# Down projection of a gated hybrid block: 25 instead of 22 groups by seven products, activation forms made after the convolution and read back from HBM, some weight sums added in place

## Chip, cores and metric

One core of one Trainium2 chip. The metric is device microseconds for one launch of the whole block; lower is better. The profile is one execution of the kernel on the chip. Engines are called as in it: PE (matmul), PEld (its weight load), DVE (vector), ACT (scalar), POOL (GpSimd), SP (which issues most transfers).

## The reference

One block with sequence 256, model width 2048 and feed-forward width 5632, all in 32-bit floats. Attention in three branches and a gate come first; the change lies in the last third:

```python
h2 = rms_norm(x, g_ffn[l])
u = causal_depthwise_conv(h2 @ w_up[l], conv_w[l], conv_b[l])   # w_up 2048 x 11264, 3 taps
u_gate, u_val = jnp.split(u, 2, axis=-1)
x = x + (jax.nn.silu(u_gate) * u_val) @ w_down[l]               # w_down 5632 x 2048
```

## The kernel before

Every 32-bit operand is split into a high and a low part that the PE reads at full rate: `hi = cast(raw)` on ACT, `lo = raw - hi` on DVE. A product of two split operands takes three matmuls (high by high, low by high, high by low; `three`, lines 1309 to 1311).

*Up projection* (lines 1219 and 1221). 176 pieces of w_up, 512 KB each, are loaded by SP (`piece`, line 172), cast (L175), subtracted (L176) and multiplied with the hidden state `hT`. After each block of rows the convolution runs on ACT and DVE (`conv`); its end is `a = silu(gate) * value`, split into `aT` (44 blocks of 128 rows; the low half at [S:]). `tick` moves such side work on by a step after each piece.

*Weight sums.* During the up projection `weight_sums` also loads w_down for the pairs that will be multiplied "by seven": four loads of 256 KB on SP's queue, three or four DVE additions (L1181), one or two stores of 512 KB to HBM on POOL's queue (L1191, L1193). A new pair starts every 7 pieces. Pairs in `ALL_FOUR` get all four sums T1 to T4 stored (two tiles), the others only T4 and T2.

*Down projection.* The output is made in two halves of 1024 columns (`nb` 0 and 1). The 44 row blocks are taken in 22 pairs per half. A pair is a 2 x 2 block product (two sequence halves t, two row blocks k, two column halves n). Done straight it has 8 products ("e", `eight`): two steps of 12 matmuls. Done by seven ("s", `seven`, Strassen's scheme in Winograd's form) it has 7 products, 21 matmuls, in four steps u0 to u3 of 3, 6, 6 and 6, and it needs

- four *forms* of the activation, sums of its blocks: `forms(p)` (five DVE operations on `aT`, L1273 to L1277, then two casts L1281, L1282 and two subtractions L1284, L1285). It runs as side work during the eights. They are kept in `sf`, in unused places of `aT`, and FS4 in the place of the block that seven products don't need;
- four *sums* of the weight: from HBM (`raw_t<-T`, `t<-T`), or for the pairs outside `ALL_FOUR` two of them added on DVE in step p2 (L1371, L1372).

The plan strings say the order, and with it the order on all queues: loads, casts, subtractions and additions are all held in program order on their engine (`keep`). `AHEAD = 2`: when step i is multiplied, the load and the split of step i+2 are emitted. The buffers are rings, and an entry is written again when its last reader is done:

- `hi` and `lo`: four entries each (`SBUFS`), so the cast of a step can start when the PE has done with the step four before it;
- `raw`: four entries of 512 KB; from the tenth load on each third load goes to `more`, two entries;
- `t13`, two entries, one for each group by seven: T1 and T3 next to each other. T4 and T2 come through `raw` or `more`.

At the end of each half `gather` and `results` add the products to the residual on DVE and store them.

Of the kernel before, what the change touches and what calls it, by code (L numbers as in the profile page):

```python
# [9 lines left out]
F32 = mybir.dt.float32  # L10
# [27 lines left out]
PLANS = ("eeeee" + "se" * 5 + "sse" + "s" + "eee", "e" + "sse" * 4 + "ssse" + "sssee")  # L38
ALL_FOUR = {(0, 6), (0, 7)} | {(1, p) for p in range(14) if p not in (4, 6, 8, 11)}
# [10 lines left out]
NSEVEN = tuple(plan.count("s") for plan in PLANS)  # L50
# [3 lines left out]
def hybrid_block(  # L54
# [1075 lines left out]
    def conv(ps, f, s):  # L1130
# [23 lines left out]
        else:  # L1154
# [9 lines left out]
            ended.append(f)  # L1164

    ended = []
    made = {}
    asked = [(0, p) for p in range(NSEVEN[0])] + [(1, p) for p in range(NSEVEN[1])]

    def weight_sums(nb, p):  # L1170
# [11 lines left out]
        four = (nb, p) in ALL_FOUR  # L1182
        add(r[0][:, 0], r[0][:, 1])
        if four:
            add(r[0][:, 1], r[1][:, 1])
# [3 lines left out]
        made[nb, p] = [dram.tile([P, PIECE], F32, name=f"T{j}_{nb}_{p}") for j in range(1 + four)]  # L1189
        if four:  # L1190
            nc.gpsimd.dma_start(made[nb, p][1], r[0].rearrange("p b n -> p (b n)"))  # L1191
# [15 lines left out]
    for f0 in range(0, FT, 4):  # L1207
        for s in range(2):
            pairs = [two_banks(f"u{f0 + i}_{s}") for i in (0, 2)]
            c0 = s * D_FF + f0 * P  # L1210
            for k in range(0, KT, 2):
# [11 lines left out]
                if asked and n_ticks[0] > 8 and n_ticks[0] % 7 == 2:  # L1223
                    adding.append([weight_sums(*asked.pop(0)), 0])
# [22 lines left out]
    FS3, FS1, FS2, FS4 = range(4)  # L1247
# [8 lines left out]
    def form_of(p, f):  # L1256
        if f == FS4:
            return pieces_of(p)[:, 0, :, 1]
        if p < 10:
            return sf[:, p, f]  # L1260
        return pieces_at(31 - p).rearrange("p k (f l q) -> p (k f) l q", f=2, l=2)[:, f]

    def forms(p):

        flat = aT[:, 2 * p : 2 * p + 3].rearrange("p k s -> p (k s)").bitcast(F32)
        v = flat[:, :1024].rearrange("p (k l t q) -> p k l t q", k=2, l=2, t=NT)
        d = sm.tile([P, 512], F32, tag="junk", bufs=2, name=f"fd_{p}").rearrange("p (f l q) -> p f l q", f=2, l=2)
        r = down_pool().tile([P, 512], F32, tag="fr", bufs=1, name=f"fr_{p}").rearrange("p (f q) -> p f q", f=4)
        g = rbc.rearrange("p (k q) -> p k q", k=2)
        two = flat[:, : 2 * 640].rearrange("p (a b) -> p a b", b=640)[:, :, :512]  # L1270
        two = two.rearrange("p a (l t q) -> p a l t q", l=2, t=NT)[:, :, :, 0]
        tt = nc.vector.tensor_tensor
        keep(tt(d, two, v[:, 0, :, 1].unsqueeze(1).to_broadcast([P, 2, 2, P]), ALU.subtract))  # L1273
# [251 lines left out]
```

## Time and profile before

| | |
|---|---|
| time of three runs | 1473.98, 1471.38, 1471.35 us; median 1471.38 |
| span of the profiled execution (first to last instruction) | 1469.9 us |
| PE busy in the span | 1462.8 us |
| granted TensorE clock, mean | 0.999 |
| up projection, about 755 to 1241 us: PE, DVE, ACT busy | 485.32, 389.15, 337.51 us |
| down projection, about 1241 to 1466 us: matmuls | 990 |

The page names no time for the profiled execution beside its span; the span is 1.5 us below the median of the runs, so what lies around it is about that. A busy PE in the profile means only that matmuls overlap; whether it runs without a gap is read from the distance between the starts of matmuls and from the list of waits.

### The profile page before, as it was taken

Reading aid. Unit: us, or ns where it says so; the run is one execution under the profiler, and the core shown is the slowest. Engines: PE = TensorE matmul, PEld = TensorE weight load, DVE = VectorE, ACT = ScalarE, POOL = GpSimd, SP = SyncE. Lnnn points to the kernel's source line nnn. Section 1 sums busy time; section 2 is a strip of 40 time slices with the busy share of each in tenths; the row PEclk is TensorE's granted clock in tenths of the full one; section 3 lists DMA queues with packets and bytes.
Section 4 is the critical chain, followed back from the end, with each engine's and each line's share of the span. In section 5 each row is a group of like instructions: output and inputs, shape, how many; then the busy total and the mean of one; then the engine's idle time right before and its main releaser. Section 6 shows DMA issues by size and latency. Waiting matters only on the chain.

```text
span 1469.9 us, 20741 instructions
## 1 busy us (share of the span) xinstructions
PE 1462.8 (100%) x7327; PEld 1233.4 (84%) x7327; DVE 1205.1 (82%) x1617; ACT 895.3 (61%) x1287; POOL 68.8 (5%) x139
## 2 busy tenths in 40 slices
PE   9999999999999999999999999999999999999998
PEld 7888888888878888888888888888888888888887
DVE  5798767766997799888877888788887886998998
ACT  6755454454664466545657667567676777665774
POOL 1000001021000000000000000000000010000000
PEclk9999999999999999999999999999999999999999
DMA  8697898787766576866776888889888895778995
GB/s 295 202 341 260 265 313 270 226 294 267 256 221 204 204 271 247 287 222 237 273 239 218 302 272 276 294 277 310 295 265 273 280 305 190 249 256 286 334 315 191
DMA packets 163463, 388.81 MB, mean 265 GB/s; under 512 B 14016, under 2 KB 22512, under 8 KB 163360
## 3 DMA queue, kind: packets, MB, share of 16 engines
q1 hardware_dynamic: 150960, 345.34, 70.6%
q0 software_dynamic: 11648, 41.10, 7.3%
q8 instruction: 57, 0.93, 0.3%
q10 hardware_dynamic: 752, 1.06, 0.2%
q14 instruction: 46, 0.38, 0.1%
HBM read 349.70 MB, written 37.75 MB: 264 GB/s over the span
## 4 chain that ended last, share of the span: by engine, by line
PE 94%; DVE 3%; DMA 2%; issue 1%; ACT 0%; SPq 0%; DVEq 0%; ACTq 0%
PE u L1219 21%; PE u L1221 10%; PE d L1310 5%; PE d L1309 5%; PE d L1311 5%; PE g_x L769 4%; PE g_x L770 4%; PE g_x L771 4%; PE s L186 2%; PE s L188 2%; PE f L187 2%; PE f L188 2%; PE f L186 2%; PE s L187 2%; PE b L186 2%; PE b L188 2%
## 5 line engine op out<-in xcount | busy, mean ns | idle before, releaser
L1219 PE MATMUL u<-hT,hi_u 128*128 128x512 f32 x1408 | 442.6, 396 | 0.0
L1221 PEld LDWEIGHTS u<-hT,lo_u 128*128 128x128 f32 x1408 | 264.4, 188 | 63.5 <-DVE lo_u L176 1.1
L1221 PE MATMUL u<-hT,lo_u 128*128 128x256 f32 x1408 | 277.0, 278 | 0.7 <-DVE lo_u L176 0.7
L176 DVE TENSOR_TENSOR lo_u<-raw_u,hi_u 128x1024 fp32r<-128x1024 f32 x176 | 213.2, 1220 | 59.8 <-ACT hi_u L175 59.0
L175 ACT CAST hi_u<-raw_u 128x1024 fp32r<-128x1024 f32 x176 | 183.0, 1049 | 107.0 <-PE u L1219 54.6
L1219 PEld LDWEIGHTS u<-hT,hi_u 128*128 128x128 f32 x1408 | 214.5, 189 | 0.1
L764 ACT CAST hi_g<-raw_g 128x1024 fp32r<-128x1024 f32 (+1 forms) x96 | 91.1, 964 | 53.5 <-PE g_x L770 33.4
L765 DVE TENSOR_TENSOR lo_g<-raw_g,hi_g 128x1024 fp32r<-128x1024 f32 (+1 forms) x96 | 105.0, 1116 | 20.9 <-ACT hi_g L764 20.8
L769 PE MATMUL g_x<-hi_g,xT 128*128 128x512 f32 x251 | 98.8, 394 | 0.0
L770 PE MATMUL g_x<-hi_g,xT 128*128 128x512 f32 x251 | 97.7, 389 | 0.0
L771 PE MATMUL g_x<-lo_g,xT 128*128 128x512 f32 x251 | 96.3, 390 | 0.0
L1148 DVE TENSOR_TENSOR y<-y,z 128x512 f32<-128x512 f32 x88 | 60.7, 691 | 24.4 <-ACT z L1147 20.5
L1147 ACT ACTIVATE z<-u,taps 128x256 f32<-128x256 f32 x176 | 74.7, 496 | 0.0
L1309 PE MATMUL d<-hi_d,aT 128*128 128x512 f32 x176 | 68.5, 389 | 0.0
L1310 PE MATMUL d<-hi_d,aT 128*128 128x512 f32 x176 | 68.5, 389 | 0.0
L1311 PE MATMUL d<-lo_d,aT 128*128 128x512 f32 x176 | 68.1, 389 | 0.0
L175 ACT CAST hi_f<-raw_f 128x1024 fp32r<-128x1024 f32 (+1 forms) x40 | 38.6, 968 | 46.6 <-PE f L187 41.9
L186 PE MATMUL s<-hi_s,xT 128*128 128x512 f32 (+1 forms) x160 | 61.9, 387 | 0.0
L175 ACT CAST hi_b<-raw_b 128x1024 fp32r<-128x1024 f32 x32 | 33.6, 1052 | 45.2 <-PE b L187 23.5
L175 ACT CAST hi_s<-raw_s 128x1024 fp32r<-128x1024 f32 (+1 forms) x40 | 38.3, 959 | 36.8 <-PE s L187 29.3
L186 PE MATMUL f<-hi_f,xT 128*128 128x512 f32 (+1 forms) x160 | 60.4, 377 | 0.0
L188 PE MATMUL s<-lo_s,xT 128*128 128x512 f32 (+1 forms) x160 | 59.1, 369 | 0.0
(498 smaller groups left out, 3265.0 us busy)
## 6 DMA issues: line engine op xcount, KB each, us to landing
raw_u<-in_w_up_dram SPq DMA_DIRECT2D x176, 512.0 KB, 5.4
raw_g<-in_w_in_dram SPq DMA_DIRECT2D x86, 512.0 KB, 5.4
T<-r POOLq DMA_DIRECT2D x64, 512.0 KB, 6.1
r<-in_w_down_dram SPq DMA_DIRECT2D x88, 256.0 KB, 5.2
raw_d<-in_w_down_dram SPq DMA_DIRECT2D x44, 512.0 KB, 5.4
raw_f<-in_w_in_dram SPq DMA_DIRECT2D x32, 512.0 KB, 5.5
raw_s<-in_w_in_dram SPq DMA_DIRECT2D x32, 512.0 KB, 5.4
raw_s<-in_w_down_dram SPq DMA_DIRECT2D x32, 512.0 KB, 5.3
```

What stands on the lines that cost most here:

```text
L175: pin(nc.scalar.copy(hi[:, :m], raw[:, :m]))
L176: pin(nc.vector.tensor_tensor(lo[:, :m], raw[:, :m], hi[:, :m].bitcast(F32), ALU.subtract))
L186: nc.tensor.matmul(o, lhsT=xh, rhs=wh, start=first, stop=False)
L188: nc.tensor.matmul(o, lhsT=xh, rhs=wl, start=False, stop=last)
L769: nc.tensor.matmul(o, lhsT=a[0], rhs=w[0], start=first, stop=False)
L770: nc.tensor.matmul(o, lhsT=a[1], rhs=w[0], start=False, stop=False)
L771: nc.tensor.matmul(o, lhsT=a[0], rhs=w[1], start=False, stop=last)
L1219: nc.tensor.matmul(ps, lhsT=hi[:, j, c], rhs=hT[:, k + j, :], start=first, stop=False)
L1221: nc.tensor.matmul(ps[:, :S], lhsT=lo[:, j, c], rhs=hT[:, k + j, :S], start=False, stop=last)
L1309: nc.tensor.matmul(o, lhsT=ah, rhs=w[0], start=first, stop=False)
L1310: nc.tensor.matmul(o, lhsT=al, rhs=w[0], start=False, stop=False)
L1311: nc.tensor.matmul(o, lhsT=ah, rhs=w[1], start=False, stop=last)
```

## The change

- 25 pairs are done by seven instead of 22: 10 in the first half, 15 in the second. Letters of the plans: `e` by eight; `f` by seven with both sum tiles read from HBM; `o` by seven with its own sums, added on DVE.
- *Forms.* The five operations on `aT` during the down projection go. After the convolution has made a pair of row blocks, `unsplit_forms` makes the four forms in three DVE operations (over 256, 128 and 128 columns) from the unsplit activation, for the first 15 pairs, and POOL's queue stores them to HBM (256 KB a pair). In the down projection they come back two pairs at a time, 512 KB through the `raw` ring, and are cast and subtracted two pairs at a time: five times in the first half, three times in the second.
- *Weight sums* during the up projection only for the 15 `f` pairs, a new pair every 9 pieces, always with four additions and both stores.
- *`o` pairs.* Their two blocks of w_down are loaded 4 steps (`LEAD`) before their step p0, into a ring `own` of two entries. Four additions make T1 to T4 from them, in program order ahead of p0's split, or one step earlier when an eight stands before the pair.
- *Buffers.* `more` and `t13` go. Both sum tiles of every pair by seven, loaded or added, lie in a new ring `sum` of two entries. `raw` keeps four entries.
- Steps p2 and p3 (with u2 and u3) change places: T1 and T3 first, then T4 and T2.

The core of the diff:

```diff
-PLANS = ("eeeee" + "se" * 5 + "sse" + "s" + "eee", "e" + "sse" * 4 + "ssse" + "sssee")
+PLANS = ("eeeee" + "fofe" + "ofe" * 3 + "o" + "eee", "e" + "offe" * 4 + "off" + "ee")
+LEAD = 4
...
             nc.vector.tensor_tensor(a[:, :, S:], g, a[:, :, :S].bitcast(F32), ALU.subtract)
             ended.append(f)
+            if f // 2 < NFORM:
+                yield 1
+                unsplit_forms(f // 2, g, y)
...
+    def unsplit_forms(p, g, y):
+        v = g.rearrange("p k (t q) -> p (k t) q", t=NT)
+        r = y.rearrange("p k (t q) -> p (k t) q", t=NT)
+        tt = nc.vector.tensor_tensor
+        tt(r[:, :2], v[:, 0:4:3], v[:, 1:2].to_broadcast([P, 2, P]), ALU.subtract)
+        nc.vector.scalar_tensor_tensor(r[:, FS2], r[:, FS1], -1.0, v[:, 0], ALU.mult, ALU.subtract)
+        tt(r[:, FS4], r[:, FS2], v[:, 2], ALU.add)
+        if p % 2 == 0:
+            rforms[p // 2] = dram.tile([P, 2, 512], F32, name=f"rform{p}")
+        nc.gpsimd.dma_start(rforms[p // 2][:, p % 2], y.rearrange("p k s -> p (k s)"))
...
-                if asked and n_ticks[0] > 8 and n_ticks[0] % 7 == 2:
+                if asked and n_ticks[0] > 8 and n_ticks[0] % 9 == 2:
...
-    def buffer(name):
-        turn[0] += 1
-        if turn[0] > 10 and turn[0] % 3 == 0:
-            return down_pool().tile([P, PIECE], F32, tag="more", bufs=2, name=name)
-        return wp.tile([P, PIECE], F32, tag="raw", name=name)
+    def buffer(name, kind):
+        if kind == "raw":
+            return wp.tile([P, PIECE], F32, tag="raw", name=name)
+        return down_pool().tile([P, PIECE], F32, tag=kind, bufs=2, name=name)
...
+    def forms(i):
+        p = 2 * i
+        n = min(2, NFORM - p)
+        raw = load(rforms[i][:, :n].rearrange("p a n -> p (a n)"), f"fr_{i}")
...
+        yield 2
+        keep(nc.scalar.copy(to[:, :, :, 0], r[:, :, :3]))
+        keep(nc.scalar.copy(last[:, :, 0], r[:, :, FS4]))
+        yield
+        keep(nc.vector.tensor_tensor(to[:, :, :, 1], r[:, :, :3], to[:, :, :, 0].bitcast(F32), ALU.subtract))
+        keep(nc.vector.tensor_tensor(last[:, :, 1], r[:, :, FS4], last[:, :, 0].bitcast(F32), ALU.subtract))
...
+    def seven(p, n0, X, Y, first, last, early):
+        own = KINDS[n0 // PIECE][p] == "o"
+        def fetch():
+            for j, k in enumerate((k0, k1)):
+                raw[j] = load(dv[:, k, n0 : n0 + PIECE], f"s{n0}_{k}", "own")
+        def sums():
+            for j in (2, 3):
+                raw[j] = buffer(f"t{j}_{name}", "sum")
+            add = lambda o, a, b: keep(nc.vector.tensor_tensor(o, a, b, ALU.add))
+            add(raw[2][:, :512], raw[0][:, :512], raw[0][:, 512:])
+            add(raw[2][:, 512:], raw[0][:, 512:], raw[1][:, 512:])
+            add(raw[3][:, 512:], raw[1][:, 512:], raw[2][:, :512])
+            add(raw[3][:, :512], raw[1][:, :512], raw[3][:, 512:])
+        if own:
+            before.setdefault(len(steps) - LEAD, []).append(fetch)
+            before.setdefault(len(steps) - early, []).append(sums)
...
         def p2():
-            raw[2] = load(made[n0 // PIECE, p][0], f"t{name}")
-            raw[3] = down_pool().tile([P, PIECE], F32, tag="t13", bufs=2, name=f"t13_{name}")
...
-            w["T4"], w["T2"] = parts(raw[2], f"t42_{name}")
+            if not own:
+                raw[2] = load(made[n0 // PIECE, p][1], f"t13_{name}", "sum")
+                raw[3] = load(made[n0 // PIECE, p][0], f"t42_{name}", "sum")
+            w["T1"], w["T3"] = parts(raw[2], f"t13_{name}")
 
         def p3():
-            w["T1"], w["T3"] = parts(raw[3], f"t13_{name}")
+            w["T4"], w["T2"] = parts(raw[3], f"t42_{name}")
...
+                seven(s, n0, X, Y, s == 0, s == ns - 1, int(plan[i - 1] == "e"))
+                if nb and s % 2 and s // 2 + 5 < (NFORM + 1) // 2:
+                    at(len(steps), lambda i=s // 2 + 5: later(forms(i)))
```

More of the change, by code (lines that the diff above doesn't have):

```diff
@@ L49 @@
 OUT_SEVENS = 3
-NSEVEN = tuple(plan.count("s") for plan in PLANS)
+KINDS = tuple(plan.replace("e", "") for plan in PLANS)
+NSEVEN = tuple(len(kinds) for kinds in KINDS)
+NFORM = max(NSEVEN)
 @with_exitstack
@@ L1188, in weight_sums @@
         add(r[1][:, 0], r[1][:, 1])
[L1189 to L1191 removed]
+        made[nb, p] = [dram.tile([P, PIECE], F32, name=f"T{j}_{nb}_{p}") for j in range(2)]
+        nc.gpsimd.dma_start(made[nb, p][1], r[0].rearrange("p b n -> p (b n)"))
         yield 1
@@ L1297, in load @@
+    def load(src, name, kind="raw"):
+        raw = buffer(f"raw_{name}", kind)
         keep(nc.sync.dma_start(raw[:, : src.shape[1]], src))
         return raw
+    def forms(i):
+        p = 2 * i
+        n = min(2, NFORM - p)
+        raw = load(rforms[i][:, :n].rearrange("p a n -> p (a n)"), f"fr_{i}")
+        r = raw.rearrange("p (a f q) -> p a f q", a=2, f=4)[:, :n]
+        to = sf[:, p % 10 : p % 10 + n]
+        last = aT[:, 2 * p : 2 * (p + n)].rearrange("p (a k) (l t q) -> p a k l t q", k=2, l=2, t=NT)[:, :, 0, :, 1]
+        yield 2
[4 more added lines that the diff above has]
+        keep(nc.vector.tensor_tensor(last[:, :, 1], r[:, :, FS4], last[:, :, 0].bitcast(F32), ALU.subtract))
+        issued.update((f"forms{p}", f"forms{p + 1}"))
@@ L1319, in f_of @@
         return to[:, 0], to[:, 1]
-    steps = []
+    steps, before = [], {}
     def eight(p, n0, X, first, last):
@@ L1348, in eight @@
         steps.append((make(k1), close if last else use(k1)))
-    def seven(p, n0, X, Y, first, last):
+    def seven(p, n0, X, Y, first, last, early):
         k0, k1 = 2 * p, 2 * p + 1
@@ L1381, in u1 @@
         def u1():
+            assert f"forms{p}" in issued
             three(X()[0][0], *a_of(k1, 0), w["10"])
@@ L1460, in hybrid_block @@
             at(-1, lambda: start(0))
+            for i in range(5):
+                at((0, 3, 6, 13, 23)[i], lambda i=i: later(forms(i)))
         for i, c in enumerate(plan):
-            if c == "s":
-                seven(s, n0, X, Y, s == 0, s == ns - 1)
+            if c != "e":
+                seven(s, n0, X, Y, s == 0, s == ns - 1, int(plan[i - 1] == "e"))
+                if nb and s % 2 and s // 2 + 5 < (NFORM + 1) // 2:
+                    at(len(steps), lambda i=s // 2 + 5: later(forms(i)))
                 s += 1
@@ L1471, in hybrid_block @@
                     at(len(steps) - 1, lambda nb=nb: residual(nb))
-                if formed < ns and n_done >= 4 - 3 * nb:
-                    at(len(steps) - 2, lambda p=formed: later(forms(p)))
-                    formed += 1
-        assert s == ns and not straight and formed >= ns
+        assert s == ns and not straight
         at(len(steps) - 1, finish)
@@ L1482, in hybrid_block, with prepare @@
         f()
-    for prep, _ in steps[:AHEAD]:
-        prep()
+    def prepare(j):
+        for f in before.pop(j, []):
+            f()
+        steps[j][0]()
+    for j in range(AHEAD):
+        prepare(j)
     for i, (_, use) in enumerate(steps):
         if i + AHEAD < len(steps):
-            steps[i + AHEAD][0]()
+            prepare(i + AHEAD)
         use()
```

61 lines of the change are left out of this document (13 added, 48 removed).

## The prediction

> **What bounds the kernel now.** I read the page first, then the PE's own waits, then the stages, then single instructions of the down projection.
>
> ```profile
> span 1469.9 us, 20741 instructions
> PE 1462.8 (100%) x7327; PEld 1233.4 (84%) x7327; DVE 1205.1 (82%) x1617; ACT 895.3 (61%) x1287; POOL 68.8 (5%) x139
> ```
>
> The list of waits, for the PE alone, and the one matmul of the up projection that waited:
>
> ```profile
> PE u L1221 <- DVE lo_u L176: 0.7, 1, 0.7
> ...
> 987.82 0.50 PE L1221 MATMUL u<-hT,lo_u 128*128 128x256 f32 x2 [0.68 <-DVE lo_u L176]
> ```
>
> The two halves of the down projection as windows (PE, PEld, DVE, ACT, POOL busy, then clock, DMA share, GB/s), and its matmuls: the count, the first start and the last start.
>
> ```profile
> 755.00:1241.00 486.00, 485.32 (x2788) 423.16 (x2787) 389.15 (x473) 337.51 (x523) 20.28 (x38) 1.00 0.83 275
> 1241.00:1353.00 112.00, 112.00 (x496) 92.79 (x496) 104.38 (x148) 70.29 (x92) 0.00 (x0) 1.00 0.74 254
> 1353.00:1466.00 113.00, 112.64 (x497) 92.95 (x496) 104.53 (x139) 70.72 (x83) 4.33 (x8) 1.00 0.81 284
> ...
> 1241.00:1466.00 225.00, 224.59 (x990) 185.74 (x990) 11.74 (x21) 1.15 (x2) 1.00 0.78 269
> ...
> 1241.05 0.40 PE L1309 MATMUL d<-hi_d,aT 128*128 128x512 f32 x1
> ...
> 1465.25 0.39 PE L1311 MATMUL d<-lo_d,aT 128*128 128x512 f32 x1
> ```
>
> From first to last start 224.20 us for 989 steps: 0.2267 us a matmul, and no wait in the list. The down projection is bound by the PE without a gap; DVE, at 104 of 112 us, is close behind. So the change can win only matmuls, and loses wherever it makes the PE wait.
>
> **The matmuls.** Three pairs go from 24 matmuls to 21: 9 x 0.2267 = 2.04 us less, all on the path.
>
> **Work of DVE and ACT.** Durations:
>
> ```profile
> L1305 DVE TENSOR_TENSOR lo_t<-t,hi_t 128x1024 fp32r<-128x1024 f32 x22 | 26.9, 1225 | 3.7 <-ACT hi_t L1304 2.6
> L1305 DVE TENSOR_TENSOR lo_s<-raw_s,hi_s 128x512 fp32r<-128x512 f32 x22 | 15.1, 685 | 0.8 <-ACT hi_s L1304 0.5 <-issue 0.3
> L1273 DVE TENSOR_TENSOR fd<-aT 128x512 f32<-128x512 f32 x14 | 9.6, 684 | 0.0
> L1275 DVE TENSOR_TENSOR fr<-fd 128x256 f32<-128x256 f32 x14 | 5.9, 418 | 0.0
> L1276 DVE SCALAR_TENSOR_TENSOR fr<-fr,rbc 128x128 f32<-128x128 f32 x14 | 4.1, 292 | 0.5
> L1284 DVE TENSOR_TENSOR sf<-fr,sf 128x384 fp32r<-128x384 f32 x10 | 5.5, 550 | 0.0
> L1285 DVE TENSOR_TENSOR aT<-fr,aT 128x128 fp32r<-128x128 f32 x14 | 4.0, 283 | 0.0
> L1304 ACT CAST hi_t<-t 128x1024 fp32r<-128x1024 f32 x22 | 23.1, 1050 | 21.8 <-PE d L1310 21.7
> ...
> L1371 DVE TENSOR_TENSOR t<-raw_s x10: 683/684/689, 1265.1 to 1438.2; 128x512 f32<-128x512 f32 x10
> ...
> L1181 DVE TENSOR_TENSOR r<-r 128x512 f32<-128x512 f32 x44 | 30.2, 686 | 0.4
> L1181 DVE TENSOR_TENSOR r<-r,r 128x512 f32<-128x512 f32 x34 | 23.3, 686 | 0.3
> ```
>
> Down projection, DVE: the five form operations go, 14 x (0.684 + 2 x 0.418 + 2 x 0.292) = 29.5 us; the form subtractions stay about as they are (14 x 0.83 before; pairs of pairs, by interpolation 0.95 + 0.42 each, 8 times at most 11); additions 40 for 20, +20 x 0.684 = 13.7; three pairs split 0.685 + 3 x 1.22 instead of 2 x 1.22, +5.7. Net some 10 us less of 209. DVE's total is not the danger; its order is (below).
>
> Up projection, DVE: additions 60 for 78, 18 x 0.686 = -12.3; forms 15 x (0.418 + 2 x 0.292) = +15.0. Net +2.7 against the 97 us it idles there (486 - 389). SP issues 60 loads of 256 KB for 88, a pair each 9 pieces for 7; POOL stores 30 sums for 34 and 15 forms of half their size. Each POOL store waits for DVE, and behind it stand only other stores; if those come late, the next sum load waits on SP, with up pieces behind it. Bounds: the 0.68 us wait above goes (-0.8), or every form costs as much as that wait did (15 x 0.68 = +10). The load on SP and the HBM shrinks, so I take -0.4.
>
> **The ring `sum`.** Here is the cost. Before, a group by seven had one of the two `t13` entries, so an entry came back two groups later. Now each group takes both. DVE, SP and ACT in one stretch:
>
> ```profile
> 1418.53 0.69 DVE L1371 TENSOR_TENSOR t<-raw_s 128x512 f32<-128x512 f32 x1
> 1419.13 0.68 DVE L1372 TENSOR_TENSOR t<-raw_s,raw_s 128x512 f32<-128x512 f32 x1
> 1419.73 1.22 DVE L1305 TENSOR_TENSOR lo_t<-raw_t,hi_t 128x1024 fp32r<-128x1024 f32 x1
> 1420.87 0.55 DVE L1284 TENSOR_TENSOR aT<-fr,aT 128x384 fp32r<-128x384 f32 x1
> ...
> 1421.69 1.23 DVE L1305 TENSOR_TENSOR lo_t<-t,hi_t 128x1024 fp32r<-128x1024 f32 x1
> ...
> 1422.95 0.33 SPq L1369 DMA_DIRECT2D t<-T  x1
> ...
> 1420.61 1.05 ACT L1304 CAST hi_t<-t 128x1024 fp32r<-128x1024 f32 x1 [1.66 <-PE d L1310]
> ...
> 1425.33 1.05 ACT L1304 CAST hi_t<-t 128x1024 fp32r<-128x1024 f32 x1 [0.30 <-PE d L1310]
> ```
>
> The split of `t` ends at 1421.69 + 1.23 = 1422.92 and the load into its entry is issued 0.03 us later: the ring holds the load. Back to back an addition takes DVE 0.60 us and a split 1.14. A cast starts when the PE gives up a `hi` entry, four steps earlier (21.7 of its 21.8 us of idle time). Landing times, least, median, most:
>
> ```profile
> L1369 SPq DMA_DIRECT2D t<-T x12: 326/426/1721, 1314.1 to 1442.7; - x12
> ...
> DMA to landing us min/median/max: 5.2/6.6/7.2
> ...
> L1297 SPq DMA_DIRECT2D raw_t<-T x22: 326/327/383, 1255.5 to 1440.7; - x22
> ...
> DMA to landing us min/median/max: 4.5/5.5/6.3
> ...
> L1297 SPq DMA_DIRECT2D raw_d<-in_w_down_dram x37: 327/332/786, 1244.9 to 1448.0; - x37
> ...
> DMA to landing us min/median/max: 3.4/5.6/8.1
> ```
>
> So one turn of a `sum` entry is load L, cast 1.05, split 1.22 and some 0.1 of hand-overs: L + 2.4. A group by seven lasts 21 x 0.2267 = 4.76 us, an eight 5.44.
>
> Take "offe", followed by the next "o", and let t = 0 be the first matmul of the "o". Its step p3 can be cast then (the eight's last step has just freed the entry), and is split at 2.4. Only then can the first "f" load T4 and T2: split at 4.8 + L. Only then can the second "f": split at 7.2 + 2L. The PE wants that low half at its last step's third matmul, 2 x 4.76 + 17 x 0.2267 = 13.37. It is late by 2L - 6.2.
>
> Behind that split stand on DVE, in program order, the split of the eight's first block (1.14), the four additions for the next "o" (4 x 0.60; they need both `sum` entries), and the split of the eight's second block (1.22): ready at 12.0 + 2L. The PE wants it at 3 x 4.76 + 14 x 0.2267 = 17.45. Late by 2L - 5.5, which takes in the lateness before it. The next "o" starts from there, so it comes again in each round.
>
> For "ofe" followed by "o": ready at 4.8 + L + 4.76, wanted at 2 x 4.76 + 3.17 = 12.69; late by L - 3.1.
>
> In the plans the first case occurs 4 times, the last "offee" (no additions) once with 2L - 6.2, the second case 4 times: 4(2L - 5.5) + (2L - 6.2) + 4(L - 3.1) = 14L - 40.6.
>
> Added to it: the first "fo", where the additions stand right behind the "f"'s last split (2.4 + 2.4 + 0.6 + 1.14 = 6.5 for a block wanted at 4.76 + 5 x 0.2267 = 5.9): 0.6. The three form loads of the second half put 1.4 us of DVE into a round each, 0 to 4.1 in all: 2. The seam of the halves, where the next "o"'s additions meet those of `gather` and `results`, 0 to 2.4: 1.2. Together about 4, from 0 to 8.
>
> L: the shortest 512 KB load in this stage took 3.4, the shortest load of a sum 4.5, their medians are 5.5 and 6.6. Those medians hold time behind a sum load issued just ahead, which the ring now keeps apart; but on SP the `own` loads of the next "o" go out between the two groups' sum loads. I take 4.5, the shortest of its own kind.
>
> - L = 4.5: 14 x 4.5 - 40.6 + 4 = 26.4.
> - L = 3.4 and no extras: 7.0. L = 5.5 and extras 8: 44.4.
>
> [...]
>
> **The sum.** -2.0 - 0.4 + 26.4 = +24.0 us. The span (1469.9) stands 1.5 below the median of the runs; what lies around it stays, so 1471.4 + 24.0 = 1495.4. Likeliest case's own range: 1471.4 + 7.0 - 2.8 = 1476 to 1471.4 + 44.4 - 2.0 = 1514. If DVE's and SP's totals alone decided, the change would win; it is the return time of one ring that turns it.
>
> **The rivals.**
>
> *The loads are hidden after all; faster.* Place: the same ring. If L were at most 2.75 in "offe" (2L = 5.5) and 3.1 in "ofe", no split came late, the 9 matmuls were won and perhaps the one wait of the up projection: 1471.4 - 2.8 = 1468.6, without the latter 1469.4. For it: the DMA has room, 0.74 and 0.81 of its time in the two halves, and DVE has less to do. Against it: no load of 512 KB landed in under 3.4.
>
> *The up projection becomes late.* Three DVE operations and a store more for each of 15 pairs; if each holds a low half as at 987.82, +10 us there. With the ring hidden it would be 1471.4 - 2.0 + 10.2 = 1479.6. Against it: 97 us of idle DVE, fewer loads on SP.
>
> *The clock falls.* After the last matmul the windows show the granted clock (the number behind the busy times):
>
> ```profile
> 1466.00:1468.00 2.00, 0.00 (x0) 0.00 (x0) 0.43 (x2) 0.00 (x0) 0.00 (x0) 1.00 0.69 241
> 1468.00:1470.00 2.00, 0.00 (x0) 0.00 (x0) 0.00 (x0) 0.00 (x0) 0.00 (x0) 0.57 0.00 0
> ```
>
> The last matmul ends at 1465.64; a mean of 0.57 over 1468 to 1470 means half clock from about 1468.3, after 2.6 us without work. If a wait in each of the five "ff" reached that and half clock held for one group, +5 x 4.76 = 24 us on top: 1519. Against it: at L = 4.5 the 3.5 us of lateness in a round come in two or three waits, each under 2.6. [...]
>
> **How the numbers follow.** A measurement of this kernel tells about 0.2%, 2.9 us, from no change. The late ring: 0.80, all of it slower. The up projection late: 0.04, slower. The clock: 0.03, slower. Hidden loads: 0.13; its best time lies 0.19% under the median, so 0.09 of it counts as the same and 0.04 as faster. That is 0.04 faster, 0.09 same, 0.87 slower. The likeliest gives 1495. For 8 in 10 I take 1476 to 1514, the likeliest case's range; it leaves out the hidden loads and the clock, and takes in the late up projection.
>
> **What would show it.** Right: the PE's waits in the down projection, none now, name `lo_t` or `hi_t` of the second "f" and `lo_d` behind the additions; the casts of the sums wait for a DMA instead of `PE d L1310`; SP waits for `lo_t` ahead of each sum load, which is issued 0.1 us after the split; an "offe" round lasts 23 to 25 us instead of 19.7; the matmuls of the down projection number 981 and keep 0.2267 within a step; the up projection ends within 1 us of 1241. Wrong: no waits of the PE there (then sum loads landed in under 3 us, or were issued before the split that I hold them to), or waits in the up projection.

## The result and the profile after

The changed kernel takes 1524.09 us (median of four runs, 1523.39 to 1528.37); the kernel before took 1472.27 (four runs, 1471.35 to 1473.98). The ratio is 1.0354, 95% interval 1.0338 to 1.037: 52 us slower. The forecast was 1495.4 us, between 1476 and 1514: slower, as forecast, but by twice as much. The profiled execution is the slowest of the four (1528.37 us, span 1526.6), so its trace holds some 4 us more than the median.

The page's head, then the PE's list of waits for the down projection, where before had none (engine, what waited, for what, then total us, times, longest):

```profile
span 1526.6 us, 20691 instructions
PE 1487.4 (97%) x7318; PEld 1235.9 (81%) x7318; DVE 1199.2 (79%) x1588; ACT 900.4 (59%) x1281; POOL 75.1 (5%) x150
```

```profile
PE d L1311 <- ACT hi_t L1306: 19.9, 14, 3.2
PE d L1311 <- ACT hi_s L1306: 4.4, 4, 2.1
PE d L1313 <- DVE lo_t L1307: 1.8, 4, 0.5
PE d L1311 <- ACT hi_d L1306: 0.9, 2, 0.6
PE d L1313 <- DVE lo_s L1307: 0.8, 2, 0.5
PE d L1313 <- DVE lo_d L1307: 0.5, 1, 0.5
```

The instructions went down as planned (9 matmuls less, 29 operations less on DVE), and the PE, which had no gap, now waits. Most of it, 19.9 of 28.3 us, is for `hi_t`, the cast of a weight sum, and that cast waits in its turn for a transfer. The list of waits of ACT and of SP says so:

```profile
ACT hi_t L1306 <- DMA raw_t<-T: 45.4, 25, 4.9
ACT hi_d L1306 <- DMA raw_d<-in_w_down_dram: 18.1, 21, 3.9
ACT hi_t L1306 <- PE d L1312: 17.6, 14, 2.5
```

```profile
SPq L1283 <- DVE lo_t L1307: 84.4, 28, 13.8
SPq L1283 <- DVE lo_s L1307: 48.6, 22, 11.0
SPq L1283 <- DVE lo_d L1307: 44.4, 20, 3.9
SPq L1283 <- DMA raw_d<-in_w_down_dram: 18.9, 6, 5.1
```

SP stands for 84 us at loads whose ring entry a split `lo_t` must free first, in 28 waits of up to 13.8 us. Before, the same queue waited for it little, and elsewhere much:

```profile
SPq L1297 <- DVE lo_d L1305: 64.5, 37, 3.9
SPq L1297 <- DVE t L1372: 42.5, 10, 5.8
SPq L1297 <- DVE lo_s L1305: 34.4, 22, 3.9
SPq L1297 <- DVE lo_t L1305: 11.5, 20, 1.2
```

A wait of SP need not cost anything: before, it stood for more than 150 us in these four rows and the PE had no gap. What is new is the length of the single waits, 13.8 and 11.0 us at the most instead of 5.8. The `lo_s` line (48.6 us, up to 11.0) is the one the prediction did not have: those are loads held for an entry of `raw` or `own`.

The down projection in numbers, from its first and last matmul and the distances between the starts of all of them:

```profile
1244.23 0.40 PE L1311 MATMUL d<-hi_d,aT 128*128 128x512 f32 x1
...
1520.73 0.39 PE L1313 MATMUL d<-lo_d,aT 128*128 128x512 f32 x1
```

It lasts 276.5 us where before took 224.2. 980 steps of 0.2267 are 222.2, so 54.3 us are lost: 38.7 in 48 gaps of more than 0.15 us (more than the 28.3 of the list, which counts a matmul as busy for some 0.4 us), 9.0 in 46 matmuls at 0.427 instead of 0.2267 (half clock), 5.7 in matmuls that start 0.1 us further apart than usual, most of them right behind a gap, 0.9 in small change. Outside of it the execution differs by 3.2 us at the start (the up projection had begun 3.6 us later in this execution; of the eleven kernels below with the same up projection eight begin the down projection between 1240.0 and 1241.8 us, none after 1243.9) and 1.3 at the end: 52.3 + 3.2 + 1.3 = 56.8, against 56.7 between the two spans.

The trace lets the loss be put to the rounds of the plan, from the first matmul of a group to the first of the next round:

| stretch | predicted late, us | measured late, us |
|---|---|---|
| first "fo": the "f" | 0.6 | 4.9 |
| "o" + "fe" in the first half, 4 rounds (unstalled 15.0 each) | 4 x 1.4 | 6.6 + 1.7 + 4.6 + 1.8 = 14.7 |
| "o" + "ffe" in the second half, 4 rounds (unstalled 19.7) | 4 x 3.5 | 7.7 + 9.4 + 5.2 + 6.6 = 28.9 |
| last "off" | 2.8 | 4.4 |
| form loads and seam | 3.2 | 1.4 (all the rest) |
| sum | 26.2 | 54.3 |

Every kind of round that the prediction had as late is late, by 1.6 to 2.6 times as much (half clock included); the first "f" by eight times. The 1.4 of the last row lie in the eight just before the first "f"; at the form loads of the second half and at the seam, for which the prediction had 3.2, nothing is lost. Inside the rounds nearly all of the loss lies in the "f" groups. The eights behind "off", for which the prediction had another 0.7 each (2L - 5.5 instead of 2L - 6.2, because of the additions on DVE), lost 0.3 in all four.

**A round as predicted, with longer loads.** SP, ACT, DVE and PE in the third "offe" round; the time is the start, the number behind it how long, in brackets the idle time before and what ended it.

```profile
1440.26 2.36 DVE L1307 TENSOR_TENSOR lo_t<-t,hi_t 128x1024 fp32r<-128x1024 f32 x2
...
1441.51 1.46 SPq L1283 DMA_DIRECT2D raw_t<-T  x2
1443.02 1.84 SPq L1283 DMA_DIRECT2D raw_s<-in_w_down_dram  x4
1447.27 4.31 SPq L1283 DMA_DIRECT2D raw_t<-T  x2
...
1448.92 1.05 ACT L1306 CAST hi_t<-raw_t 128x1024 fp32r<-128x1024 f32 x1 [2.94 <-DMA raw_t<-T]
...
1454.71 1.05 ACT L1306 CAST hi_t<-raw_t 128x1024 fp32r<-128x1024 f32 x1 [2.78 <-DMA raw_t<-T]
...
1450.02 0.50 PE L1311 MATMUL d<-hi_t,sf 128*128 128x512 f32 x1 [1.53 <-ACT hi_t L1306]
...
1455.81 0.50 PE L1311 MATMUL d<-hi_t,sf 128*128 128x512 f32 x1 [1.83 <-ACT hi_t L1306]
```

The two splits of the "o" (from 1440.26) free the `sum` entries; SP issues the first "f"'s loads at 1441.51 and 1442.64, in each case 0.03 us after a split. They land after 3.3 and 6.2 us. Behind them SP lets out the next group's four `raw` and `own` loads in one go (1443.02, x4). The second "f"'s loads wait for the first "f"'s splits, go out at 1447.27 and 1451.25, and land after 7.3 and 5.3 us; the four loads ahead of the first of them land at 1449.51, 1450.77, 1452.06 and 1453.33. The casts start 0.1 us after the landings, at 1448.92 for the first "f"'s second sum tile and at 1454.71 for the second "f"'s first, and the PE stands 1.53 and 1.83 us for them.

**A round the prediction did not have.** At the first "f" the `sum` ring is still empty, nothing holds its two loads, and yet the PE stands 2.07 and 0.53 us:

```profile
1261.64 9.11 SPq L1283 DMA_DIRECT2D raw_s<-in_w_down_dram  x4
1270.80 0.90 SPq L1283 DMA_DIRECT2D raw_t<-T  x2
...
1268.09 1.05 ACT L1306 CAST hi_d<-raw_d 128x1024 fp32r<-128x1024 f32 x1 [3.85 <-DMA raw_d<-in_w_down_dram]
1274.91 1.05 ACT L1306 CAST hi_s<-raw_s 128x1024 fp32r<-128x1024 f32 x1 [2.25 <-DMA raw_s<-in_w_down_dram]
...
1269.17 1.23 DVE L1307 TENSOR_TENSOR lo_d<-raw_d,hi_d 128x1024 fp32r<-128x1024 f32 x1 [4.72 <-ACT hi_d L1306]
...
1276.01 0.50 PE L1311 MATMUL d<-hi_s,aT 128*128 128x512 f32 x1 [2.07 <-ACT hi_s L1306]
```

The last of the four loads of the first row is the "f"'s second block. It needs the `raw` entry that the split at 1269.17 gives up at 1270.40, and is issued at 1270.42; both sum loads, which had their entries, stand behind it on SP until 1270.80. That split was itself late because its load, issued at 1261.27 between a form load and two `own` loads, took 6.7 us. Few entries, one queue in program order: the loads came in bursts, the six that SP issued from 1259.53 to 1270.42 landed after 4.4 to 9.2 us, and the late one held the next burst.

### The profile page after: what moved, and what is told of

The parts are those of the page before. It is cut to its first block, busy times and chain, and to the rows that moved or that the text cites. A ratio compares the mean times of both kernels' runs of the same rounds, so it can differ in the third digit from the quotient of the medians.

```text
span 1526.6 us, 20691 instructions
## 1 busy us (share of the span) xinstructions
PE 1487.4 (97%) x7318; PEld 1235.9 (81%) x7318; DVE 1199.2 (79%) x1588; ACT 900.4 (59%) x1281; POOL 75.1 (5%) x150
## 4 chain that ended last, share of the span: by engine, by line
PE 72%; DMA 11%; DVE 8%; issue 5%; ACT 3%; SPq 0%; POOL 0%; DVEq 0%; ACTq 0%; POOLq 0%
PE u L1235 17%; PE u L1237 8%; PE g_x L771 4%; PE g_x L772 4%; PE g_x L773 4%; DMA raw_t<-T 3%; DMA raw_d<-in_w_down_dram 2%; PE f L188 2%; PE f L189 2%; PE f L190 2%; PE b L189 2%; PE b L188 2%; PE b L190 2%; PE d L1313 1%; PE o_x L773 1%
## 5 line engine op out<-in xcount | busy, mean ns | idle before, releaser
L767 DVE TENSOR_TENSOR lo_g<-raw_g,hi_g 128x1024 fp32r<-128x1024 f32 (+1 forms) x96 | 105.0, 1117 | 19.7 <-ACT hi_g L766 19.5
L1307 DVE TENSOR_TENSOR lo_t<-raw_t,hi_t 128x1024 fp32r<-128x1024 f32 x30 | 36.8, 1225 | 42.0 <-ACT hi_t L1306 41.6
L1307 DVE TENSOR_TENSOR lo_d<-raw_d,hi_d 128x1024 fp32r<-128x1024 f32 x38 | 46.2, 1222 | 20.8 <-ACT hi_d L1306 18.6
L1306 ACT CAST hi_t<-raw_t 128x1024 fp32r<-128x1024 f32 x30 | 31.4, 1048 | 51.5 <-DMA raw_t<-T 45.4
L177 ACT CAST hi_b<-raw_b 128x1024 fp32r<-128x1024 f32 x32 | 33.5, 1054 | 46.2 <-PE b L189 30.5
L1311 PE MATMUL d<-hi_d,aT 128*128 128x512 f32 x152 | 59.7, 392 | 0.9 <-ACT hi_d L1306 0.9
```

The source lines that it names most:

```text
L177: pin(nc.scalar.copy(hi[:, :m], raw[:, :m]))
L767: pin(nc.vector.tensor_tensor(lo[:, :n], src, hi[:, :n].bitcast(F32), ALU.subtract))
L1307: keep(nc.vector.tensor_tensor(lo[:, :n], src, hi[:, :n].bitcast(F32), ALU.subtract))
```

## Experiments

All times are medians beside runs of the kernel before on the same chip (1471.5 to 1472.5). "Lost" is worked out as above from the distances of the matmuls' starts. The runs are numbered in the order of the record, not of this text: e1 and e7 have four `sum` entries, e2 half of the sums through `raw`, e3 the sum loads twice, e4 no additions, e5 the forms alone, e6 the plan with the rings of before, e8 later forms in `frm`, e9 the own loads last, e10 and e12 the forms in one entry on SP and on POOL, e11 and e13 the sum loads on POOL, e14 24 groups, e15 and e16 three entries, e17 no two "f" in a row. Where a part of the output is left out, the text or the expectation says so.

**Does the `sum` ring decide? Four entries.** Two kernels. In the first `own` is given up for it, and the own blocks go through `raw`:

```diff
-        return down_pool().tile([P, PIECE], F32, tag=kind, bufs=2, name=name)
+        return down_pool().tile([P, PIECE], F32, tag=kind, bufs=4, name=name)
-                raw[j] = load(dv[:, k, n0 : n0 + PIECE], f"s{n0}_{k}", "own")
+                raw[j] = load(dv[:, k, n0 : n0 + PIECE], f"s{n0}_{k}")
```

> The changed kernel with one ring resized: `sum` gets four entries instead of two. The memory comes from the ring `own`, which goes; the own blocks of the `o` pairs are loaded through `raw` (four entries) instead. Theory A (the return time of a `sum` entry, landing + cast + split, holds the next group's loads): with four entries an entry comes back a group later, most of the waits of the PE in the down projection go (54 us of extra time there now), 1472 to 1482 us. Rival B (the additions standing on DVE ahead of the eight's second split): they stand where they stood, 1510 or more. Rival C (`raw` shrank from six entries to four and holds the forms too): it gets more crowded, 1524 or more.

Measured: 1533.49 us, ratio 1.0418 (1.0388 to 1.0449). SP now waits at `raw`:

```profile
SPq L1283 <- DVE lo_d L1307: 79.9, 31, 5.3
SPq L1283 <- DVE lo_s L1307: 62.6, 47, 3.8
```

Theory A's 1472 to 1482 failed. Room in one ring was bought with crowding in another and the sum was worse, so this run says nothing on the `sum` ring alone; it says that `raw` has no room to give. The second kernel keeps `own` and `raw`:

```diff
-        return down_pool().tile([P, PIECE], F32, tag=kind, bufs=2, name=name)
+        return down_pool().tile([P, PIECE], F32, tag=kind, bufs=4 if kind == "sum" else 2, name=name)
```

> The clean form of the ring test, since e1 also moved the own blocks into `raw`: `sum` with four entries, `own` and `raw` as in the change. The memory comes from the residual, whose four rows share one tile here, so the residual part of the output is left out of its right place and the first half's stores come after its four additions. Theory A (the return of a `sum` entry): 1472 to 1482 us. Theory D, formed from e1, e4 and e5 (SP issues in order, and loads of all rings wait for splits made at most a few steps before, so a load freed early still stands behind one that is held; `raw` with four entries and the forms in it is as tight as `sum`): 1495 to 1515.

Measured: 1506.43 us, 1.0234 (1.0215 to 1.0253), where theory D had it and not theory A. 18 of the 52 us go with the return of the `sum` entries. The collapsed residual does not give them: e8 has it too, with two `sum` entries, and is no faster than the change. What the PE still waits for:

```profile
PE d L1311 <- ACT hi_t L1306: 12.3, 6, 4.3
PE d L1311 <- ACT hi_s L1306: 2.6, 2, 2.1
PE d L1313 <- DVE lo_t L1307: 2.1, 4, 0.5
```

Sum loads again, although SP's waits at `lo_t` fell to 13.0 us: now SP stands at `lo_s`, and the sum loads land after 6.6 us on average.

```profile
SPq L1283 <- DVE lo_s L1307: 79.3, 41, 10.7
...
SPq L1283 <- DVE lo_t L1307: 13.0, 10, 2.5
```

**Half of the sums through `raw`.** T4 and T2 of the "f" groups:

```diff
-                raw[3] = load(made[n0 // PIECE, p][0], f"t42_{name}", "sum")
+                raw[3] = load(made[n0 // PIECE, p][0], f"t42_{name}")
```

> The changed kernel, but the tile T4/T2 of an `f` pair is loaded through `raw` (as before the change) and only T1/T3 through `sum`, which keeps its two entries. Theory A: an `f` takes one `sum` entry, so the second `f` of "off" no longer waits for the first; most waits go, 1475 to 1490 us. Rival B: 1510 or more. Rival C: two more loads in each "off" for the four entries of `raw`, 1524 or more.

Measured: 1517.52 us, 1.031 (1.028 to 1.034), 7 us better than the change. Theory A's 1475 to 1490 failed. The `sum` ring is relieved, `raw` carries more; a small net gain.

**Three entries, and the forms out of the way.** Between two and four, and then with the form loads (one of 256 KB a pair) on POOL's queue in an entry of their own, so that they take nothing of `raw` or SP:

```diff
-        return down_pool().tile([P, PIECE], F32, tag=kind, bufs=2, name=name)
+        return down_pool().tile([P, PIECE], F32, tag=kind, bufs=3 if kind == "sum" else 2, name=name)
# in the second kernel also
-        raw = load(rforms[i][:, :n].rearrange("p a n -> p (a n)"), f"fr_{i}")
+        raw = down_pool().tile([P, 512], F32, tag="fr", bufs=1, name=f"fr_{p}")
+        keep(nc.gpsimd.dma_start(raw, rforms[p // 2][:, p % 2]))
```

> The change with three `sum` entries instead of two; `own` and `raw` as in the change; the residual rows share one tile so that the third entry has room (part of the output is left out, as in e7_sum4own). Ring theory: the lateness of the second "f" falls from two turns of the ring to little over one, so most of what four entries gave (1506) is there: 1506 to 1513. If the order on SP and not the number of entries decides, it stays within 4 us of 1524.

> e15_sum3, and the form loads (one of 256 KB for a pair) go on POOL's queue into an entry of their own, so that none of them takes an entry of `raw` and none stands on SP. Theory that the forms in `raw` are the next limit once `sum` has room: 10 to 15 us under e15_sum3, as the same move gave 21 where the entry was the limit; near 1496. Rival, that what is left lies in `own` and `raw` without the forms: within 4 us of e15_sum3.

Measured: 1518.23 (1.0312, 1.0295 to 1.033) and 1516.68 (1.0302, 1.0282 to 1.0322). The third entry gives 6 us, the fourth another 12; the first of these results lies between its two forecasts. One entry more does not yet uncouple two groups (the table by rounds below shows it). Taking the forms out of `raw` gives nothing in sum; the expectation of 10 to 15 us failed. SP still stands at the same places in the second kernel:

```profile
SPq L1284 <- DVE lo_s L1306: 80.1, 26, 13.6
SPq L1284 <- DVE lo_t L1306: 67.9, 19, 13.7
```

A sister of it gives nothing in sum either: the form loads of the change, from the fourth on, in an entry of their own on SP, with two `sum` entries.

```diff
-        raw = load(rforms[i][:, :n].rearrange("p a n -> p (a n)"), f"fr_{i}")
+        raw = load(rforms[i][:, :n].rearrange("p a n -> p (a n)"), f"fr_{i}", "frm" if i > 2 else "raw")
```

> The changed kernel with the later form loads (from the fourth on) in an entry of their own instead of `raw`; `sum` keeps two entries. Residual collapsed as in e7, so the same part of the output is left out. Theory A: `raw` is not the place, 1518 to 1525 us. Theory D: a form load holds one of four `raw` entries for four steps, five times in this kernel from the fourth on, 2 to 3 us each: 1508 to 1516.

Measured: 1526.75 (1.0372, 1.0353 to 1.0391), as the change.

**No two "f" in a row.** 22 groups, the number of before; the rest as in the change:

```diff
-PLANS = ("eeeee" + "fofe" + "ofe" * 3 + "o" + "eee", "e" + "offe" * 4 + "off" + "ee")
+PLANS = ("eeeee" + "fofe" + "ofe" * 3 + "o" + "eee", "e" + "ofe" * 5 + "of" + "eeee")
```

> The change with 22 groups by seven instead of 25 (the number of before): the second half has "ofe" five times, then "of", so that no two "f" stand together; rings, forms and queues as in the change. Ring theory: the five cases of 2L fall away, nine of L - 3.1 stay, with the landing of 5.9 that the changed kernel shows 25 us, and 1 to 4 us of half clock: 1471.4 + 25 + 3 = 1499; with the 11 to 13 us that the forms cost by themselves up to 1511. If "ff" is not the worst place, the time stays within 5 us of 1524.

Measured: 1513.37 us, 1.0278 (1.0263 to 1.0293). 11 us less than the change, of which the fewer groups take 2 away again: the second "f" costs 13 us, the formula with the landing of the changed kernel (5.6) gives 4 x 5.7 + 5.0 - 5 x 2.5 = 15. It is the worst place but not the greater part: 40.2 us are still lost (30.5 in gaps, 5.5 at half clock, the rest behind gaps). The nine "ofe" rounds hold 31.2 of them, where nine times L - 3.1 with that kernel's median of 5.8 is 24; the first "f" and the eight before it hold 7.1, which the formula does not have. The forecast of 1499 to 1511 was just missed; its landing of 5.9 is 5.6 over all 30 sum loads of the changed kernel.

**No additions for the "o" groups.** The four additions are left out and the "o" takes no `sum` entry:

```diff
-            before.setdefault(len(steps) - early, []).append(sums)
...
+            if own:
+                raw[2], raw[3] = raw[0], raw[1]
```

> The changed kernel without the additions of the `o` pairs: their four sums are left out, the unsummed blocks are multiplied in their place, and the `o` pairs take no `sum` entry. Theory A: the first `f` finds both entries free, the return from the first to the second `f` stays (five times, late by 9.5 + 5.7 - 13.4 = 1.8 us each), 1478 to 1488 us. Rival B: the additions were the cause, nothing is left, 1469 to 1474. Rival C: nothing of `raw` changes, 1515 or more.

Measured (one run): 1509.83 us. Only 14 us better although one group of two or three leaves the ring and 27 us of DVE go; 31.6 us of gaps remain. So these gaps do not come from the additions, and the forecast of 1478 to 1488 failed. The table shows where.

**The loss by rounds.** For the profiled execution of each kernel, by the starts of the matmuls as above (us, half clock included); e15 and e7 have three and four `sum` entries, e4 has no additions, e16 is e15 with the forms out of the way.

| kernel | first "f" | four rounds "ofe" | first "f" of five "off" | second "f" of five "off" | all the rest | sum |
|---|---|---|---|---|---|---|
| the change | 4.9 | 14.7 | 10.8 | 22.0 | 1.9 | 54.4 |
| e15 | 5.1 | 16.4 | 0.5 | 21.1 | 1.4 | 44.5 |
| e7 | 6.0 | 13.4 | 0.0 | 12.3 | 0.6 | 32.3 |
| e4 | 4.0 | 21.5 | 0.0 | 11.6 | 2.9 | 40.0 |
| e16 | 0.0 | 22.1 | 0.0 | 22.9 | 0.3 | 45.2 |

In "off" the loss does what the return of a `sum` entry asks: a third entry frees the first "f" and leaves the second, a fourth halves the second. Without the "o" in the ring (e4) the first "f" is free and the second loses 2.3 us each time, where theory A had 1.8. That theory failed in the "ofe" rounds, for which it had nothing. There the own blocks are held until p3; whether that is the reason was not tried. And in e16 the first "f" of all loses nothing: the form loads were what held it (their entry, queue, size and time changed together). As much is lost again in its "ofe" rounds, for a reason that no run shows.

**A load that costs more: each sum load issued twice.**

```diff
+                    keep(nc.sync.dma_start(raw[j], made[n0 // PIECE, p][i]))
```

> The changed kernel with each load of a sum tile in the down projection issued twice into the same entry, so that every return takes one more transfer (about 1.28 us) and nothing else changes. Theory A: the sum of the prediction has 14 returns on the path, so 14 x 1.28 = 18 us more, 1542, up to 1555 if the clock falls oftener. Rivals B and C: the path does not go through these loads, under 5 us more.

Measured (one run): 1628.42 us, +104 to the change, about 3.5 us for each of the 30 loads added. The second load writes the same entry and is issued 0.02 us after the first has landed (1272.40, then 1272.42), so a sum costs two landings one after the other, 4.97 and 3.13 us for the first pair, and the loads behind it on SP wait as well:

```profile
PE d L1311 <- ACT hi_t L1306: 86.7, 30, 6.9
```

Each of the 30 sum loads has a wait of the PE now; what is added to the landing of a sum comes back nearly one for one (half clock included), and the plan has no slack for it. The expectation had mis-sized what was added: it counted a transfer and not a landing.

**What stands behind a held load: the order on SP.** The same change to before (the forms via HBM, no other part), one load of 256 KB a pair into one small entry, once on SP's queue and once on POOL's:

```diff
+        raw = down_pool().tile([P, 512], F32, tag="fr", bufs=1, name=f"fr_{p}")
+        keep(nc.sync.dma_start(raw, rforms[p // 2][:, p % 2]))      # the second kernel: nc.gpsimd
```

> The kernel before with the forms made after the convolution and read back from HBM, as e5, but each pair's forms in a transfer of 256 KB into an entry of their own (2 KB a partition, the place of the old form scratch) and at most one at a time, instead of two pairs at a time through `raw` and `more`. Theory D: e5's 13 us came from the form loads in the ring of raw tiles, so this is back within 2.9 us of before, 1469 to 1475. If they came from the work in the convolution or from the traffic itself, it stays at 1480 or more.

> e10 (kernel before, forms through HBM into one entry of their own) with the form loads on POOL's queue. In e10 SP waited 98 us in all, 12 times, for that entry. Theory D: the form load now waits where nothing stands behind it, back to 1470 to 1476. If the traffic or the casts of the forms are the cost, 1490 or more.

Measured: 1504.55 (1.0214, 1.02 to 1.0228) and 1483.03 (1.0074, 1.0061 to 1.0087). The same 14 loads, the same entry: 21.5 us between the queues. SP's list of the first, POOL's row in the list of the second:

```profile
SPq L1296 <- DVE aT L1304: 98.1, 12, 10.0
```

```profile
POOL fr L1296 <- DVE aT L1304: 133.1, 9, 64.2
```

Both wait about 100 us or more for the one entry. On POOL no weight load stands behind; on SP all of them do, and go out in bursts when the entry is free. In the first kernel the PE waits for `hi_s` (7.5) and `hi_d` (4.6), which have nothing to do with the forms:

```profile
PE d L1316 <- ACT hi_s L1311: 7.5, 4, 3.9
PE d L1316 <- ACT hi_d L1311: 4.6, 3, 2.2
```

The second lies between its two forecasts: the queue is the greater part of the cost of the first, and 11.5 us are left. Three more runs bear on the order. With the own loads put behind the other loads of their step:

```diff
+        late = []
         for f in before.pop(j, []):
-            f()
+            late.append(f) if f.__name__ == "fetch" else f()
         steps[j][0]()
+        for f in late:
+            f()
```

> The changed kernel with one order changed on SP's queue: the two own loads of the next `o` are emitted behind the loads of their step instead of ahead of them, so behind the two sum loads of the `f`. Theory A: the sum loads have up to 2 x 1.28 us less in front of them in eight rounds, 1505 to 1515 us. Theory D: what is taken from one load is given to another, the own blocks then wait behind held sum loads and the additions come later, 1518 to 1535.

Measured: 1542.9 us (1.0482, 1.0462 to 1.0501), 19 worse than the change; the SP wait at `lo_t` rises to 134.6 us, and the own loads, which had room, now stand behind sum loads that had none. The additions come late, as theory D had it, though its 1518 to 1535 was too low: the eights behind the first "f" lose 15.1 us in all instead of the change's 0.8. With the sum and form loads on POOL's queue:

```diff
-        keep(nc.sync.dma_start(raw[:, : src.shape[1]], src))
+        keep((nc.gpsimd if kind == "sum" or name[:2] == "fr" else nc.sync).dma_start(raw[:, : src.shape[1]], src))
```

> The changed kernel with the loads of the sum tiles and of the forms issued on POOL's queue instead of SP's; rings and program order as in the change. Theory A (only the return of a `sum` entry): the entry still comes back when the split ends, the waits stay, 1515 or more. Theory D (a held load on the in-order queue stops the loads behind it, of other rings too): the held sum loads stop only each other, 1485 to 1505.

> e7 (`sum` with four entries, residual collapsed, so that part of the output is left out) with the sum and form loads on POOL's queue as in e11. Theory D with A: neither the return within a pair of groups nor the queue is left, 1474 to 1490. If it stays at e7's 1506, the queue is not the second cause.

Measured: 1555.13 (1.0567, 1.0545 to 1.0588) with two `sum` entries, 1507.66 (1.0244, 1.0225 to 1.0263) with four. With two it is 31 us worse than the change (POOL's waits, then the issues of 22 of the 30 sum loads, those from 1241 to 1480 us, with size and median landing):

```profile
POOL raw_t L1283 <- DVE lo_t L1307: 171.1, 22, 22.1
```

```profile
raw_t<-T POOLq DMA_DIRECT2D x22, 512.0 KB, 7.9
```

The ring holds the sum loads on POOL as it did on SP; freed of them SP runs ahead with the weights, and the sums land behind those, after 7.1 us (median of all 30) instead of 5.6. Theory D's 1485 to 1505 failed here, and its 1474 to 1490 in the other kernel. With four entries the queue makes no difference (1506.43 on SP). So the order on SP is harmful where a held load stands ahead of others that could go; it is not the limit of the sum loads themselves.

**The forms by themselves and the plan by itself.** Before with the forms via HBM, two pairs a load through `raw` and `more`, the rings and the 22 groups of before:

```diff
+        raw = load(rforms[i][:, :n].rearrange("p a n -> p (a n)"), f"fr_{i}")
```

> The kernel before with one part of the change alone: forms made after the convolution for its 14 pairs, stored to HBM and read back two pairs at a time, seven loads, through the buffers of before (`raw` and `more`). Plans, weight sums and rings as before. Theory A: the forms are harmless, within 2.9 us of before (1469 to 1474), with the one wait of the up projection (0.8 us) perhaps moved. Rival C (form loads crowd the ring of raw tiles): waits of the PE at the steps behind form loads, 5 us or more.

Measured: 1485.07 us, 1.01 (1.0083 to 1.0116): the forms alone cost 13 us, with e12's 11.5 in the kindest way tried. In e12 the PE's list for the two last stages is

```profile
PE u L1240 <- DVE lo_u L178: 3.2, 2, 2.4
PE d L1316 <- ACT hi_t L1311: 2.1, 1, 2.1
```

The prediction had the up projection at -0.4 and the forms at some 2 us. Then the 25 groups with e5's forms and the rings and sums of before (a pair of sums every 6 pieces of the up projection, no `own`), and 24 groups with e12's forms:

```diff
-PLANS = ("eeeee" + "se" * 5 + "sse" + "s" + "eee", "e" + "sse" * 4 + "ssse" + "sssee")
+PLANS = ("eeeee" + "sse" * 4 + "ss" + "eee", "e" + "ssse" * 4 + "sss" + "ee")
```

> 25 groups by seven (plans eeeee sse sse sse sse ss eee and e ssse ssse ssse ssse sss ee) and the forms from the convolution, but with the rings of before: T4/T2 through `raw` and `more`, `t13` two entries, one for each group, no ring `own`; four pairs of the second half and six of the first add T1 and T3 on DVE in step p2 as before; 25 weight sums in the up projection, one each 6 pieces. Theory A: no ring returns within a group, so 9 matmuls less, -2.0 us: 1468 to 1471. If instead 25 groups in themselves are too many for DVE or the DMA, the PE waits in the rows of three or more groups by seven: 1475 or more.

> A version meant to beat both: the kernel before with 24 groups by seven (9 and 15), its own rings, weight sums each 7 pieces, and the forms from the convolution through one entry on POOL's queue as in e12. Six matmuls fewer are -1.4 us; two weight sums and 15 stores of forms more in the up projection, 0 to +4. Theory D: 1469 to 1476; if three groups by seven in a row are too much for the rings of before, 1480 or more.

Measured: 1491.26 (1.0134, 1.0115 to 1.0152) and 1487.11 (1.0107, 1.0091 to 1.0122). Neither forecast of 1468 to 1471 and 1469 to 1476 held. 25 groups with even more neighbouring groups lose only 12.1 us in the down projection (9.8 in gaps, none at half clock) when the rings are those of before; what they lose besides is in the up projection, which must make more sums: its end moves to 1249.3 (PE for `lo_u` 4.8 us, 6 waits). So the change's down projection suffers from its rings and from what goes through them, not from the number of groups. No version tried is faster than before.

## Why the prediction was right in direction and wrong in size

- *"What bounds the kernel: the PE without a gap; the change can win only matmuls and loses wherever the PE waits."* Right: 981 matmuls, 0.2267 us apart within a step, and all of the loss is gaps and their consequences.
- *"The ring holds the load; a turn is L + 2.4."* Right as a mechanism: the loads of sums leave 0.03 us after a split, 25 of the 30 casts wait for the transfer instead of the PE, and the list names `hi_t` and `lo_t`. Four entries took away 18 us, leaving out neighbouring "f"s 13. The sign "`lo_d` behind the additions" hardly came: 0.5 us, once.
- *L = 4.5: the step that failed first, a term of the sum that was mis-sized.* Sum loads landed after 3.1 at the least, 5.6 in the median and on average, 9.0 at the most. The last lines of that view, for the sum loads of the changed kernel:

```profile
L1283 SPq DMA_DIRECT2D raw_t<-T x30: 326/326/424, 1270.8 to 1500.8; - x30
...
DMA to landing us min/median/max: 3.1/5.6/9.0
```

  I took the shortest of before because the ring would keep the sum loads apart. It does, but it makes the other loads come together: the next group's `raw` and `own` loads leave in one burst between them. With 5.6 the same formula gives 14 x 5.6 - 36.6 = 41.8, so 1471.4 - 2.4 + 41.8 = 1510.8, inside the range that I gave (its upper bound was worked out with 5.5 and larger extras). That 41.8 comes near the 45.3 us lost without half clock (54.3 - 9.0) is in part luck: the sum has 0.6 instead of 4.9 for the first "f" and some 2.5 too much for the eights behind "off", and for the kernel without neighbouring "f"s it gives 24 where the same rounds lost 31.2. The 5.6 is read from the changed kernel itself, so this is an account afterwards and no test. Four of the 30 sum loads landed after 3.1 to 3.3 us, the other 26 after 4.5 to 9.0.
- *"Only the sum ring holds": failed.* The first "f", with an empty `sum` ring, was put at 0.6 and lost 4.9; `hi_s`, `lo_s`, `hi_d`, `lo_d` together make some 11 of the 38.7 us of gaps. The prediction counted the freed DMA time and SP's instructions, but not that six entries (`raw`, `more`) shrank to four while the form loads came in, nor that a load held on SP holds every load behind it. With the form loads elsewhere (e16) the first "f" lost nothing. e10 against e12 shows the price of a held load on SP by itself, 21.5 us, on the kernel before; for the change no run gives it (e13 is as slow as e7, e11 slower than the change).
- *The clock, given 0.03: it happened.* Seven times in the down projection, 9.0 us. I priced it as one wait of 2.6 us in each "ff". The trace has a fall, at 1505.73, after 3.41 us in which the longest wait was 1.56 us, and none at the wait of 1.83 us up to 1455.81; see the last section.
- *Up projection -0.4, hidden loads, DVE's totals.* The up projection waits 0.3 us for `lo_u` once where before it waited 0.7; the loads were not hidden. With the forms alone on before it can be late by 2 to 3 us (e12), so this rival was real but small. DVE's time fell by 5.9 us (some 7 by the sums), and bought nothing.

What is shown: the return of `sum` entries (18 us, e7), the order on SP and the forms' own cost on the kernel before (21.5, e10 and e12; 11 to 13, e5 and e12), the clock (9.0, in part within the others). These overlap and are not a sum to 52. What stays open: of the 34 us left with four `sum` entries, which share is `raw` with four entries, which the forms in it and which `own`. e16 shows that the forms held the first "f" (4.9 us), and that moving them does not help in sum with three entries; four entries with the forms moved as in e16 were not tried, nor were more `raw` and `own` entries beside four of `sum`.

## What to carry to other kernels

When a ring gets fewer entries, price its turn with the landing time that a load has behind the loads it will be issued with, not the shortest of the trace; here that one number is the difference between 1495 and 1511 in the sum; what leads from there to 1524 is half clock and loads held in other rings. On a queue that is kept in program order, look at every load whose entry may not be free: here SP stood up to 13.8 us at one, with loads of other rings behind it; the four behind the sum loads of 1441.51 and 1442.64 left in a burst and landed after 6.5 to 8.9 us. In this kernel, where the PE had no gap, a matmul is 0.2267 us, and one late round eats ten of them (L - 3.1 = 2.5 us at 5.6).

## What the runs showed of the hardware

*Landings of one burst.* In the "ofe" round from 1284.7 on, six loads of SP landed at 1291.27, 1292.87, 1294.16, 1295.44, 1296.72 and 1298.00, the last five 1.28 us apart, in the order of issue, whichever ring they belong to (512 KB each: `own`, two sums, two of an eight, forms). The shortest sum load landed after 3.1 us; the last of these six, issued at 1289.85, after 8.1.

*The clock in the changed kernel.* In the down projection the granted clock fell to 0.50 at 1277.04, 1294.11, 1331.65, 1393.09, 1430.64, 1481.84 and 1505.73 us, each time for 3.41 us. Counted at 0.2267 us each, matmuls fill 0.26 to 1.38 us of the 3.41 before each fall. Two stretches of that length, each with the one that follows it (PE busy with its count, granted clock, DMA share, GB/s):

```profile
1454.53:1457.94 3.41, 2.07 (x7) 1.00 0.93 311
1457.94:1461.35 3.41, 3.35 (x14) 1.00 0.55 219
1502.32:1505.73 3.41, 1.79 (x8) 1.00 0.87 261
1505.73:1509.14 3.41, 3.41 (x10) 0.50 0.98 344
```

The stretch before 1505.73 held a wait of 1.56 us and some 1.4 us of matmuls, and the next one ran at half clock. The stretch from 1454.53 held the greater part of the wait of 1.83 us shown above (up to 1455.81) and a little more work, and the clock stayed at 1.00. So the clock stayed at the longer of the two waits; why was not shown.

*Split parts and 32-bit operands.* In the profile before, at granted clock 1.00, a matmul over 512 columns of split parts is followed by the next after 0.23 us (749.22 to 749.45). Eight transposes of 128 columns of 32 bits each (L215, from 750.38 on) take 0.80 us to the next start, 0.40 for 512 columns.
